# First loads of an encoder layer in halves over two queues, and one accumulating transfer in place of two

## Chip, cores and metric

The kernel runs on one core of one Trainium2 chip. The metric is device microseconds of one execution, taken over several runs. The engines are named as in the profile: PE is the matmul engine, PEld its weight load, DVE the vector engine, ACT the scalar engine, POOL the general-purpose engine, SP the engine that here only issues transfers. A name with a trailing q (SPq, ACTq, POOLq) is the instruction queue of that engine.

## What is computed

One layer of an encoder trunk over 512 positions and 1024 channels, in float32:

```python
def swiglu(h, w_gate, w_up, w_down):
    return (jax.nn.silu(h @ w_gate) * (h @ w_up)) @ w_down

x = x + 0.5 * swiglu(rms_norm(x, ffn1_norm), ffn1_w_gate, ffn1_w_up, ffn1_w_down)
h = rms_norm(x, mix_norm)
u = h @ w_in
f_out = fourier_mixer(u[..., :o0], fnet_w, fnet_b)
a_out = gqa_attention(u[..., o0:o1], u[..., o1:o2], u[..., o2:], q_norm, k_norm)
x = x + jnp.concatenate([f_out, a_out], axis=-1) @ w_out
x = x + 0.5 * swiglu(rms_norm(x, ffn2_norm), ffn2_w_gate, ffn2_w_up, ffn2_w_down)
return rms_norm(x, final_norm)
```

The inner width of both feed-forward parts is 2752, which is 21 blocks of 128 and one of 64.

## The kernel before

Activations lie transposed: `x[k]` is channel block k (128 partitions) by 512 positions, and all of x, after 32 columns of gains, is one tile `gx`. For precision each float32 operand of a matmul is split into a high part, rounded to the matmul's format, and a low part, the remainder. A product of two split operands takes three matmuls (high by high, high by low, low by high). The high part is made by ACT (a cast), the low part by DVE (line 141, a subtraction), or, for some tiles, by a transfer: in `rest_by_dma` ACT writes the negated high part into the low tile (line 172) and POOL issues a transfer from the raw float32 data that adds to it (line 175), in `pieces` column pieces. Split weights lie in slots of one tile, `ring`.

**The opening.** Line 749 on, before the first feed-forward part. `raws[i]` (tile `raw_first`) holds, for two channel blocks, the first four 128-wide chunks of the gate and up weights: [128, 2, 4, 128]. ACT issues two transfers for `raws[0]` (line 751), one for each channel block, 256 KB each. PE runs nine matmuls on a constant (line 757, tile `busy`). SP issues x in five blocks (`load_x`, line 770): block 0 is the gains and `x[0]` (272 KB), block 1 is `x[1]` (256 KB), blocks 2 to 4 are two channel blocks each (512 KB), and in between the weights `raws[1]` to `raws[3]` (line 776, 512 KB each). In `opening1`, for each channel block k, `highs` makes the high parts of x (line 225 on DVE for k = 0, line 227 on ACT otherwise) and of the weights (line 798 on ACT; for k = 0 in two halves, chunks 0 to 1 and chunks 2 to 3), DVE makes the low parts (lines 231 and 141), and `products(k)` issues twelve matmuls (line 812): four chunks high by high, then four high by low, then four low by high. The order of ACT and DVE in the opening is written out by hand; the order of PE and SP is that of the program. What is not written out is ordered by a planner from modelled costs.

**The feed-forward parts.** `ffn` runs four groups of inner blocks. The first group, two or three blocks and the 64-wide rest, is computed plainly by `gate` (lines 201 and 187). The later groups go by `seven`: for each inner block, gate and up are computed as a two-by-two block product with seven multiplications instead of eight. `prepare(j)` returns the steps that make a block's seven weight operands: `ld` (SP loads `raw_g` and `raw_u`, line 398), `a.h` (the high parts of a11 and a12, ACT, line 409), `a.l` (their low parts, `low`, by `rest_by_dma` in two pieces of 256 KB: one for a11, one for a12), `c1` to `c4` (sums on DVE, line 424), and so on. A product `P0` to `P9` is four pairs of matmuls (lines 454 and 457). `P0` uses a11, so it reads what the first piece of `a.l` wrote; `P1` uses a12.

After each group its down projection runs (tile `dn`, line 201; weights from `raw_dn`, cast at line 187). While the down projection of a group runs, the steps of the first block of the next group are issued ahead, in program order between its rounds (`ahead`), and the load of the second block:

```python
if d == (1 if gi else 2) and not last:
    ready = [prepare(groups[gi + 1][0] + i) for i in (1, 2)]
    ahead.extend(ready[0][n] for n in FIRST)
    ahead.append(ready[1]["ld"])
```

So there are six first blocks, three in each feed-forward part. In the middle of the kernel the mixing stage runs in an order written out by hand for all engines. The program gives the transfers of SP and ACT eight completion counters in turn, so that the issue of the ninth waits until the first has landed.

Of the kernel before, what the change touches and what calls it, by code (L numbers as in the profile page):

```python
# [15 lines left out]
P = 128  # L16
S = 512
D = 1024
KD = D // P
# [21 lines left out]
HALF = S // 2  # L41
# [53 lines left out]
def asf(ap):  # L95
    return ap.bitcast(F32)
# [3 lines left out]
def encoder(ctx, tc, A, out):  # L100
    nc = tc.nc
# [18 lines left out]
    def bank(name):  # L120
        return pp.tile([P, S], F32, tag="bank", name=name)


    gx = cp.tile([P, 4 * KD + KD * S], F32, name="gx")
    gains = gx[:, : 4 * KD].rearrange("p (n k) -> p n k", k=KD)
    xt = gx[:, 4 * KD :].rearrange("p (k s) -> p k s", s=S)
    x = [xt[:, k, :] for k in range(KD)]
# [12 lines left out]
    def lows(lo, src, hi):  # L140
        return nc.vector.tensor_tensor(out=lo, in0=src, in1=asf(hi), op=ALU.subtract)  # L141
# [28 lines left out]
    def rest_by_dma(lo, hi, src, pieces=1):  # L170

        nc.scalar.activation(lo, asf(hi), AF.Copy, scale=-1.0)  # L172
        n = lo.shape[-1] // pieces
        for c in (slice(i * n, (i + 1) * n) for i in range(pieces)):
            nc.gpsimd.dma_start(out=lo[..., c], in_=src[..., c], accum_op=ALU.add)  # L175
# [123 lines left out]
    def ffn(norm, after, wgu, wd, wdt, groups, opening, closing):  # L299
# [6 lines left out]
        with tc.tile_pool(name=f"act{n_}", bufs=1) as ap, tc.tile_pool(name=f"sums{n_}", bufs=2) as sp:  # L306
# [5 lines left out]
            wt, raws = [], {}  # L312
# [61 lines left out]
            def back(ts):  # L374
                plain[:] = [t for t in plain if all(t is not q for q in ts)]

            def take():

                t = next(t for t in own or plain if any(t is q for q in own or shared))
                for q in own, shared:  # L380
                    q[:] = [p for p in q if p is not t]
                taken.append(t)
                return t
# [3 lines left out]
                    taken[:] = [q for q in taken if q is not t]  # L387
                    (shared if any(t is q for q in slots[KD:]) else own).append(t)

            def prepare(j):  # L390

                ops, w, t = {}, {}, {}

                def load():
                    t["g"] = sp.tile([P, KD * P], F32, tag="raw_g", name=f"raw_g{n_}_{j}")
                    t["u"] = wp.tile([P, KD * P], F32, tag="raw", name=f"raw_u{n_}_{j}")
                    for r, c in ((t["g"], 2 * j), (t["u"], 2 * j + 1)):
                        nc.sync.dma_start(out=r.rearrange("p (a b) -> p a b", b=P), in_=wgu[c])

                def high(names, src):  # L400
                    if len(names) == 2:
                        hi, lo = (take() for _ in range(2))
                        last = max(names, key=USES.index)
                        w[last, "slots"] = hi, lo
                    else:
                        both = take()
                        hi, lo = both[:, :S], both[:, S:]
                        w[names[0], "slots"] = (both,)
                    nc.scalar.copy(hi, src())  # L409
                    for i, n in enumerate(names):  # L410
                        w[n] = tuple(t[:, i * S : (i + 1) * S] for t in (hi, lo))
                    t[names] = lo, hi

                def low(names, src):
                    lo, hi = t[names]
                    if names[0] in BY_DMA:
                        rest_by_dma(lo, hi, src(), 2)
                    else:
                        lows(lo, src(), hi)

                def combine(tag, c, a, b, op):
                    if c == 0:
                        t[tag] = sp.tile([P, 2 * S], F32, tag=tag, bufs=1, name=f"{tag}_{n_}_{j}")
                    nc.vector.tensor_tensor(out=t[tag][:, c : c + S], in0=a(), in1=b(), op=op)

                a11, a12, a21, a22, s1, s2, s3 = (
                    (lambda r=r, c=c: t[r][:, c : c + S])
                    for r, c in (("g", 0), ("g", S), ("u", 0), ("u", S), ("s12", 0), ("s12", S), ("s34", 0))
                )
                for k, names, src in (  # L430
                    ("a", ("a11", "a12"), lambda: t["g"]), ("s", ("s1", "s2"), lambda: t["s12"]), ("d", ("a22",), a22),
                    ("t", ("s3", "s4"), lambda: t["s34"]),
                ):
                    ops[f"{k}.h"] = lambda names=names, src=src: high(names, src)
                    ops[f"{k}.l"] = lambda names=names, src=src: low(names, src)
                ops["c1"] = lambda: combine("s12", 0, a21, a22, ALU.add)
                ops["c2"] = lambda: combine("s12", S, s1, a11, ALU.subtract)
                ops["c3"] = lambda: combine("s34", 0, a11, a21, ALU.subtract)
                ops["c4"] = lambda: combine("s34", S, a12, s2, ALU.subtract)
                ops["ld"] = load  # L440
                return {**ops, "w": w}
# [165 lines left out]
            def by_tokens(ps, c, group):  # L607

                t = slice(c * P, (c + 1) * P)
                for i in range(LAST):  # L610
                    nc.tensor.matmul(
                        ps[:, i * P : (i + 1) * P], x[KD - LAST + i][:, t], ident, is_transpose=True,
                        start=i == 0, stop=False, skip_group_check=True,
                    )
                for j in group:
                    h, l = (at[:, where[j], o, t] for o in range(2))
                    whi, wlo = (w[:, j - group[0]] for w in tw)
                    for a, b in ((h, whi), (l, whi), (h, wlo)):
                        nc.tensor.matmul(
                            turned(ps[:, : LAST * P]), a, turned(b), start=False, stop=j == group[-1] and b is wlo,  # L620
                            skip_group_check=True,
                        )
                    yield
# [16 lines left out]
            for gi, group in enumerate(groups):  # L640
# [9 lines left out]
                else:  # L650
# [9 lines left out]
                    for i, c in enumerate(left):  # L660
                        pss.setdefault(c // 2, []).append(gate(c, by_dma=i in (1,) if n_ else i > 0))
                        if due:
                            j = due.pop(0)
# [20 lines left out]
                for d in range(KD):  # L684
                    if last and closing and d == KD - LAST:
                        closing(
                            [(e, down(e, group, gi)) for e in range(d, KD)], residual,
                            lambda ps, c: by_tokens(ps, c, group), finished,
                        )
                        break  # L690
                    if last and d == KD - 2:
                        back(lent)
                    ps = bank(f"dn{n_}_{d}_{gi}")
                    while len(downs) < min(d + 1 + (0 if gi or not n_ else 2), KD):
                        downs.append(behind(lambda: down(len(downs), group, gi)))
                    steps = downs[d](ps, every)
                    for _ in range(len(group) - (last and d < 2) - HELD * (d == KD - 1 and not last)):
                        next(steps)
                    waiting.append((d, ps, steps))
                    if d == (1 if gi else 2) and not last:  # L700
                        ready = [prepare(groups[gi + 1][0] + i) for i in (1, 2)]
                        ahead.extend(ready[0][n] for n in FIRST)
                        ahead.append(ready[1]["ld"])
                    if d == 0:
                        rest()
                        if last:

                            lent = slots[KD - 2 : KD]
                            plain[0:0] = lent
                            continue  # L710
                    def finish(waiting=waiting, added=added if last or d < KD - 1 else lambda d, ps: residual(d, ps, every)):
                        for d_, ps, steps in waiting:
                            for _ in steps:
                                pass
                            added(d_, ps)

                    if d < KD - 1 or last:
                        finish()
                    waiting = []
# [27 lines left out]


    raws = [wp.tile([P, 2, 4, P], F32, tag="raw", name=f"raw_first{i}") for i in range(KH)]
    for a in range(2):  # L750
        nc.scalar.dma_start(out=raws[0][:, a], in_=A["first0"][a])


    one = [nc.const_aps.tensor(1.0, [P, n], BF16) for n in (P, S)]
# [7 lines left out]

    n0, n1 = Norm(0), Norm(1)

    cut = [0] + [4 * KD + k * S for k in (1, 2, 4, 6, 8)]

    def load_x(i):
        a, b = cut[i : i + 2]
        src = A["x"][a * P : b * P].rearrange("(p n) -> p n", p=P)
        nc.sync.dma_start(out=gx[:, a:b], in_=src)  # L770

    load_x(0)
    load_x(1)
    for i in range(1, KH):
        load_x(i + 1)
        nc.sync.dma_start(out=raws[i], in_=A["first"][i - 1])
# [74 lines left out]
    with tc.tile_pool(name="mix", bufs=1) as mp, tc.tile_pool(name="mixt", bufs=1) as mt:  # L851
# [49 lines left out]
        raws, ws = {}, {}  # L901
# [757 lines left out]
```

## Time and profile before

| | us |
|---|---|
| median of 3 runs | 813.91 (813.85 to 814.01) |
| the profiled execution's own time | 813.67 |
| its span, first to last instruction | 811.9 |
| PE busy | 805.0 (99% of the span) |
| DVE busy | 642.5 (79%) |
| ACT busy | 546.7 (67%) |
| POOL busy | 109.3 (13%) |

Times in the views are microseconds from the start of the span. The profiled execution's time is 1.8 us more than its span, and 0.24 us under the median of the runs. A busy PE is counted from the start to the modelled end of its matmuls, which overlap; what counts here is where it is not busy. In a view of the timeline a row gives start, length, engine, line, operation, the tile written and the tiles read, how many instructions were merged, and in brackets the idle time before the row and what ended it.

### The profile page before, as it was taken

The page shows a single profiled execution, that of the slowest core. Times are in us where ns is not written, and L with a number is a line of the kernel's source. Part 1 is how long each engine was busy: PE and PEld are TensorE (multiplying, and loading weights), DVE is VectorE, ACT ScalarE, POOL GpSimd, SP SyncE. Part 2 cuts the span into 40 slices and gives each one's busy share as a digit, 9 for nine tenths or more (in the row PEclk, how much of TensorE's full clock was granted, in tenths as well). Part 3 has the DMA queues.
Part 4 walks back from the last instruction along what each step waited for, and adds up shares of the span by engine and source line. Part 5 has one row for each costly group of instructions (what it writes and reads, how often), then busy time and mean ns, then how long its engine had stood idle before and what let it go on. Part 6 is the DMA issues. An engine that isn't in the chain of part 4 may idle for free.

```text
span 811.9 us, 11937 instructions
## 1 busy us (share of the span) xinstructions
PE 805.0 (99%) x4376; PEld 705.4 (87%) x4376; DVE 642.5 (79%) x1077; ACT 546.7 (67%) x871; POOL 109.3 (13%) x124
## 2 busy tenths in 40 slices
PE   9999999999999999999999999999999999999997
PEld 7888988888888888889988888888888888889887
DVE  7996998389765967799998588989883998489774
ACT  7774876278635845779999557568743876278562
POOL 0120220022001200211000001212100220022001
PEclk9999999999999999999999999999999999999999
DMA  7775875558474743352110316678573785558432
GB/s 260 176 164 167 182 175 154 158 136 187 125 208 95 144 125 117 105 172 80 55 52 27 105 52 162 139 195 199 114 208 105 173 185 141 163 130 180 112 97 104
DMA packets 44955, 114.25 MB, mean 141 GB/s; under 512 B 5216, under 2 KB 10720, under 8 KB 44896
## 3 DMA queue, kind: packets, MB, share of 16 engines
q1 hardware_dynamic: 25184, 75.33, 29.8%
q0 software_dynamic: 16400, 29.90, 20.9%
q10 hardware_dynamic: 3312, 8.26, 3.3%
q8 instruction: 34, 0.56, 0.3%
q14 instruction: 25, 0.20, 0.1%
HBM read 84.24 MB, written 2.10 MB: 106 GB/s over the span
## 4 chain that ended last, share of the span: by engine, by line
PE 92%; DVE 4%; DMA 2%; issue 1%; ACT 1%; POOLq 0%; POOL 0%; DVEq 0%; ACTq 0%
PE dn L201 25%; PE r L454 15%; PE mix L201 9%; PE r L457 8%; PE p L454 4%; PE c L454 4%; PE q L454 4%; PE gu L201 3%; PE gu L812 3%; PE p L457 2%; PE q L457 2%; PE c L457 2%; PE mix L1312 2%; PE mix L1272 2%; PE mix L1110 1%
## 5 line engine op out<-in xcount | busy, mean ns | idle before, releaser
L201 PE MATMUL dn<-at,ring 128*128 128x512 f32 x900 | 203.5, 380 | 0.3 <-ACT ring L187 0.3
L201 PEld LDWEIGHTS dn<-at,ring 128*128 128x128 f32 x900 | 167.6, 188 | 29.6 <-ACT ring L187 0.7
L454 PE MATMUL r<-rt,ring 128*128 128x512 f32 x560 | 190.8, 382 | 0.0
L457 PE MATMUL r<-rt,ring 128*128 128x256 f32 x560 | 153.0, 273 | 0.0
L454 PEld LDWEIGHTS r<-rt,ring 128*128 128x128 f32 x560 | 105.1, 188 | 18.7
L457 PEld LDWEIGHTS r<-rt,ring 128*128 128x128 f32 x560 | 105.2, 188 | 0.4
L175 POOL DMA_DIRECT2D ring<-raw_g x70 | 61.0, 1026 | 274.9 <-ACT ring L172 143.0
L635 DVE SCALAR_TENSOR_TENSOR gx<-dn,gx 128x512 f32<-128x512 f32 x61 | 41.7, 686 | 66.3 <-PE dn L201 66.3
L141 DVE TENSOR_TENSOR ring<-s,ring 128x1024 fp32r<-128x1024 f32 x70 | 85.3, 1219 | 2.5 <-ACT ring L409 0.6
L409 ACT CAST ring<-s 128x1024 fp32r<-128x1024 f32 x70 | 73.0, 1043 | 7.8 <-PE p L454 5.6
L187 ACT CAST ring<-raw_dn 128x768 fp32r<-128x768 f32 (+3 forms) x58 | 44.9, 780 | 48.8 <-PE dn L201 35.9
L141 DVE TENSOR_TENSOR ring<-raw_dn,ring 128x768 fp32r<-128x768 f32 (+3 forms) x58 | 51.4, 891 | 15.4 <-ACT ring L187 14.5
L172 ACT ACTIVATE ring<-ring 128x1024 fp32r<-128x1024 f32 x38 | 40.3, 1060 | 14.2 <-PE dn L201 12.5
L201 PE MATMUL gu<-ring 128*128 128x512 f32 x216 | 48.9, 381 | 0.0
L454 PE MATMUL p<-rt,ring 128*128 128x512 f32 x140 | 48.5, 382 | 0.0
L454 PE MATMUL q<-rt,ring 128*128 128x512 f32 x140 | 48.3, 382 | 0.0
L454 PE MATMUL c<-rt,ring 128*128 128x512 f32 x140 | 48.3, 382 | 0.0
L490 ACT COPY p<-r 128x512 f32<-128x512 f32 x35 | 19.9, 570 | 41.2 <-PE r L457 41.2
L201 PEld LDWEIGHTS gu<-ring 128*128 128x128 f32 x216 | 40.4, 188 | 6.9
L409 ACT CAST ring<-raw_g 128x1024 fp32r<-128x1024 f32 x35 | 36.7, 1049 | 11.3 <-DMA raw_g<-in_wgu 11.2
L457 PE MATMUL p<-rt,ring 128*128 128x256 f32 x140 | 38.3, 274 | 0.0
L457 PE MATMUL q<-rt,ring 128*128 128x256 f32 x140 | 38.2, 273 | 0.0
(284 smaller groups left out, 1685.2 us busy)
## 6 DMA issues: line engine op xcount, KB each, us to landing
raw_g<-in_wgu SPq DMA_DIRECT2D x35, 512.0 KB, 4.1
raw_u<-in_wgu SPq DMA_DIRECT2D x35, 512.0 KB, 5.3
ring<-raw_g POOLq DMA_DIRECT2D x70, 256.0 KB, 6.4
raw_dn<-in_wd SPq DMA_DIRECT2D x25, 384.0 KB, 3.3
raw_gu<-in_wgu SPq DMA_DIRECT2D x12, 512.0 KB, 3.6
at<-u POOLq DMA_DIRECT2D x23, 256.0 KB, 3.3
raw_dn<-in_wd ACTq DMA_DIRECT2D x15, 384.0 KB, 3.3
raw_o<-in_wo SPq DMA_DIRECT2D x8, 512.0 KB, 3.4
```

The lines of the kernel that those rows point to most:

```text
L141: return nc.vector.tensor_tensor(out=lo, in0=src, in1=asf(hi), op=ALU.subtract)
L172: nc.scalar.activation(lo, asf(hi), AF.Copy, scale=-1.0)
L175: nc.gpsimd.dma_start(out=lo[..., c], in_=src[..., c], accum_op=ALU.add)
L187: cast["ACT"] = nc.scalar.copy(hi[:, :n, :], raw[:, :n, :])
L201: nc.tensor.matmul(ps, a, b, start=first and b is mhi and a is whi, stop=last and a is wlo)
L409: nc.scalar.copy(hi, src())
L454: nc.tensor.matmul(turned(ps), whi[:, ks], turned(m), start=first and i == 0, stop=False, skip_group_check=True)
L457: nc.tensor.matmul(turned(ps[:, :HALF]), wlo[:, ks], turned(m[:, :HALF]), start=False, stop=i == KH - 1, skip_group_check=True,)
L490: nc.scalar.copy(o[key], o["r"])
L635: nc.vector.scalar_tensor_tensor(out=x[d][:, t], in0=ps[:, t], scalar=0.5, in1=x[d][:, t], op0=ALU.mult, op1=ALU.add)
L812: nc.tensor.matmul(turned(pss[c]), w[:, k % 2, c], turned(m[k]), start=k == 0 and m is hh and w is hi, stop=k == KD - 1 and w is lo,)
L1272: nc.tensor.transpose(pts[n][:, c * P : (c + 1) * P], prob[t, b, c][:, kc * P : (kc + 1) * P], ident)
```

## The change

Two edits.

In the opening, block 0 of x with the gains and the first channel block of `raws[0]` are each cut in two. SP issues the gains with the first 256 positions of `x[0]` (144 KB), then chunks 0 to 1 of the weights (128 KB). ACT issues the other 256 positions (128 KB), then chunks 2 to 3 (128 KB), and then, as before, the second channel block of `raws[0]` (256 KB). `load_x` moves up in the text and gets the queue and the columns as arguments. The rest of the loads follow in the same order as before.

In `prepare`, the first of the two blocks that are prepared ahead (i = 1) has its `a.l` in one transfer of 512 KB instead of two of 256 KB. This holds for the six first blocks; all others keep two.

```diff
-            def prepare(j):
+            def prepare(j, early=False):
...
-                        rest_by_dma(lo, hi, src(), 2)
+                        rest_by_dma(lo, hi, src(), 1 if early else 2)
...
-                        ready = [prepare(groups[gi + 1][0] + i) for i in (1, 2)]
+                        ready = [prepare(groups[gi + 1][0] + i, i == 1) for i in (1, 2)]
...
     raws = [wp.tile([P, 2, 4, P], F32, tag="raw", name=f"raw_first{i}") for i in range(KH)]
-    for a in range(2):
-        nc.scalar.dma_start(out=raws[0][:, a], in_=A["first0"][a])
+    cut = [0] + [4 * KD + k * S for k in (1, 2, 4, 6, 8)]
+
+    def load_x(i, by=nc.sync, t=slice(0, None)):
+        a, b = cut[i : i + 2]
+        src = A["x"][a * P : b * P].rearrange("(p n) -> p n", p=P)
+        by.dma_start(out=gx[:, a:b][:, t], in_=src[:, t])
+
+    early = slice(0, 4 * KD + HALF), slice(4 * KD + HALF, None)
+    for by, t, c in zip((nc.sync, nc.scalar), early, (slice(0, 2), slice(2, 4))):
+        load_x(0, by, t)
+        by.dma_start(out=raws[0][:, 0, c], in_=A["first0"][0][:, c])
+    nc.scalar.dma_start(out=raws[0][:, 1], in_=A["first0"][1])
...
-    cut = [0] + [4 * KD + k * S for k in (1, 2, 4, 6, 8)]
-
-    def load_x(i):
-        a, b = cut[i : i + 2]
-        src = A["x"][a * P : b * P].rearrange("(p n) -> p n", p=P)
-        nc.sync.dma_start(out=gx[:, a:b], in_=src)
-
-    load_x(0)
     load_x(1)
     for i in range(1, KH):
         load_x(i + 1)
```

## The prediction

> **What bounds the kernel now.** I read the page's shares first, then the chain that ended last, then the waits of PE, and then the opening by timeline. The page:
>
> ```profile
> span 811.9 us, 11937 instructions
> PE 805.0 (99%) x4376; PEld 705.4 (87%) x4376; DVE 642.5 (79%) x1077; ACT 546.7 (67%) x871; POOL 109.3 (13%) x124
> ```
>
> PE is idle for 6.9 us in all. Busy time in stretches (start and end, length, then PE busy) says where:
>
> ```profile
> 0.00:5.03 5.03, 3.82 (x9) 1.17 (x10) 0.84 (x7) 1.95 (x4) 0.70 (x6) 1.00 0.64 200
> 5.03:28.00 22.97, 22.97 (x109) 19.49 (x110) 19.98 (x30) 18.39 (x30) 1.53 (x1) 1.00 0.72 253
> 345.00:500.00 155.00, 154.92 (x897) 136.53 (x896) 130.91 (x237) 123.69 (x225) 9.70 (x9) 1.00 0.27 86
> 500.00:800.00 300.00, 299.72 (x1643) 264.20 (x1642) 236.25 (x388) 194.84 (x298) 45.88 (x52) 1.00 0.61 148
> 800.00:811.90 11.90, 6.60 (x44) 6.27 (x43) 4.89 (x11) 2.55 (x7) 2.86 (x5) 0.91 0.49 176
> ```
>
> Idle are 1.21 us in the opening, 0.36 us from 5.03 to 800, and 5.3 us in the tail, which the change does not touch. So what moves the first product moves the end by as much, and between the opening and the tail there is next to nothing to win. The first entries of the chain (start, length, what) and the waits of PE over the whole kernel:
>
> ```profile
> 0.74 3.81 DMA raw_first<-in_first
> ...
> 4.57 0.41 ACT ring L798
> ...
> 5.03 17.89 PE gu L812 x80
> ...
> PE busy L757 <- PEq L1642: 0.8, 1, 0.8
> PE gu L812 <- ACT ring L798: 0.4, 1, 0.4
> PE dn L201 <- ACT ring L187: 0.3, 1, 0.3
> ```
>
> The opening is bounded by the landing of the first weights and their cast, and the constant matmuls before it cap the gain:
>
> ```profile
> 0.78 3.82 PE L757 MATMUL busy<-const-bfloat16-1.0 128*128 128x512 bf16 x9 [0.78 <-PEq L1642]
> 4.40 0.48 DVE L225 TENSOR_SCALAR ring<-gx 128x512 fp32r<-128x512 f32 x1 [3.28 <-DMA gx<-in_x]
> 4.57 0.71 ACT L798 CAST ring<-raw_first 128x256 fp32r<-128x256 f32 x2 [1.41 <-DMA raw_first<-in_first]
> 5.51 0.72 ACT L227 ACTIVATE ring<-gx 128x512 fp32r<-128x512 f32 x1 [0.23 <-DMA gx<-in_x]
> ```
>
> The nine end at 4.60. The high part of x is done at 4.88, the first half cast at 4.98, the first product starts at 5.03. The gap is 0.43 us, so the first product can come at most 0.43 us earlier, 0.05% of the time. About 0.2% (1.6 us) is what a measurement of this kernel can tell from no change.
>
> **The opening, by bytes.** Before, ACT's first transfer (262 kB, rows of 2 KB) and SP's first (279 kB, rows of 2176 B) run at once. After, each queue has half of x and then half of the weights: SP 147 + 131 kB, ACT 131 + 131 kB. That is the same count of bytes on each queue ahead of the last byte needed. x lands earlier, but the cast that was last waits for the weights, which now come second. The issue costs nothing itself: SP's second issue starts some 0.4 us after its first, long before the first one's bytes have gone. What remains is the rate, since the rows are now 1024 and 1152 B. Three stretches, with the busy share of the transfer engines and the GB/s at the end of the row: 3 to 4 us (rows of 2 KB, the opening), 6 to 8 us (rows of 4 KB), and 497.5 us, where only a transfer of 1 KB rows runs (`raw_dn`, 128 KB):
>
> ```profile
> 3.00:4.00 1.00, 1.00 (x4) 0.31 (x3) 0.00 (x0) 0.16 (x1) 0.00 (x0) 1.00 1.04 394
> 6.00:8.00 2.00, 2.00 (x10) 1.69 (x9) 1.84 (x4) 1.47 (x3) 0.00 (x0) 1.00 1.01 412
> 497.50:498.00 0.50, 0.50 (x4) 0.44 (x3) 0.50 (x2) 0.50 (x2) 0.00 (x0) 1.00 0.66 205
> q1 hardware_dynamic: 109, 0.20, 54.1%
> q10 hardware_dynamic: 106, 0.19, 49.6%
> ```
>
> The last two rows are the queues of SP and ACT between 3 and 4 us: they share the engines evenly, so neither half overtakes the other by its queue. At a full share, rows of 1 KB run at 205 / 0.66 = 311 GB/s. The 541 kB take 1.37 us at 394 GB/s and 1.74 us at 311; the 147 kB in rows of 1152 B are a little quicker, so I count 1.72 us, 0.35 us more.
>
> The Trainium skill, "DMA: Bandwidth & Descriptors", section "Why small descriptors are slow (HBM only)", puts the price at about 3 cycles of bus a packet beside one for each 32 B: an estimate of 35/67 for 1 KB against 2 KB, 4.5% a byte, or 0.06 us here, by which the sum would be about 0.15 us earlier than before. The trace disagrees: from 2 KB to 1 KB rows the rate falls by 21%.
>
> Where the SP half landed, if bytes alone counted: x block 0 was issued at 0.74 and landed 3.6 us later:
>
> ```profile
> gx<-in_x SPq DMA_DIRECT2D x1, 272.0 KB, 3.6
> gx<-in_x SPq DMA_DIRECT2D x1, 256.0 KB, 4.2
> raw_first<-in_first ACTq DMA_DIRECT2D x2, 256.0 KB, 4.2
> ```
>
> So SP's half of the weights, which ends the same 279 kB, lands at 4.34 at the old rate and at 4.69 at the new. The cast of half the weights takes 0.41 us (4.57 to 4.98) and PE follows 0.05 later: 4.82 or 5.17. That is -0.21 or +0.14 us. I take +0.1, near the dearer value, because its row is of the same row length. The bounds: below, -0.43 (the constant matmuls). Above, the halves land like the transfer that was issued second on SP before (`x[1]`, issued at about 1.15, 4.2 us to landing, 5.37): cast to 5.78, product at 5.83, +0.80. ACT's half, 4.55 + 0.35 = 4.90, is cast behind the first half (which ends at 5.10), and is wanted two matmuls after the first product, 0.44 us later: hidden.
>
> **What else the opening moves.** One more issue on ACT (0.45 us) lies ahead of its table load; ACT was idle for 1.41 us before the cast, so it is covered. SP's later loads come behind one more issue, and in the new order the ninth transfer is `x` block 3 instead of block 4; the wait of the ninth for the first, seen before, moves there:
>
> ```profile
> SPq L770 <- DMA raw_first<-in_first: 0.8, 1, 0.8
> 2.60 0.62 SPq L770 DMA_DIRECT2D gx<-in_x  x1
> 3.26 0.46 SPq L776 DMA_DIRECT2D raw_first<-in_first  x1
> 4.56 0.33 SPq L770 DMA_DIRECT2D gx<-in_x  x1
> 12.36 0.71 ACT L227 ACTIVATE ring<-gx 128x512 fp32r<-128x512 f32 x1
> 12.97 0.60 ACT L798 CAST at<-raw_first 128x512 fp32r<-128x512 f32 x1
> ```
>
> Block 3 would be issued at some 3.9 (when the first half of x lands) instead of 2.60, `raws[2]` at some 4.7 instead of 3.26, block 4 at some 5.1 instead of 4.56. Queued behind are only loads; the bytes ahead of them, 1.6 MB on SP's queue and 0.5 MB on ACT's, keep the engines full until about 8 us, so a later issue leaves no hole. Their first users stand at 12.36 and 12.97. If that cover were gone, 1.3 us of delay would stand against the 0.43 us gap of the first wait. The nearest users are tighter: `x[1]` is scaled at 5.51 after a wait of 0.23 for its landing, and its weights are cast until 6.74, while PE reaches channel block 1 at 5.03 + 12 x 0.22 = 7.7. Delayed by the 0.35 us of the rate, 0.6 us are left. DVE's first three steps start earlier or wait for the same cast.
>
> **The six accumulating transfers.** The edit takes out 6 of 70 issues on POOL (about 0.87 us each) and a landing each. POOL is 13% busy. One transfer of 512 KB was seen only from the weights in memory: 5.3 and 5.7 us to landing. The pairs took, by the group and by single places:
>
> ```profile
> ring<-raw_g POOLq DMA_DIRECT2D x70, 256.0 KB, 6.4
> ring<-in_wgu POOLq DMA_DIRECT2D x3, 512.0 KB, 5.3
> at<-in_wgu POOLq DMA_DIRECT2D x1, 512.0 KB, 5.7
> 523.12 1.78 POOL L175 DMA_DIRECT2D ring<-raw_g  x2 [10.54 <-ACT ring L187]
> L175 POOL DMA_DIRECT2D ring<-raw_g x2: 900/1038/1176, 523.1 to 523.7; - x2
> DMA to landing us min/median/max: 3.4/4.2/5.0
> 533.80 0.38 PE L454 MATMUL r<-rt,ring 128*128 128x512 f32 x1
> 534.02 0.27 PE L457 MATMUL r<-rt,ring 128*128 128x256 f32 x1
> ```
>
> The last five rows are of the tightest of the six places, the second group of the second feed-forward part: issue at 523.12, first piece down 3.4 us later, the second 5.0 us after its own issue at 523.7. P0 starts at 533.80 and its first matmul with the low part at 534.02. So the first piece had 7.5 us to spare, and one piece that takes 5.7 us has 5.2. `raw_g` comes free at about 528.8 instead of 528.7, so the next load of SP, which waits for it, moves by a tenth either way. Cost: zero, hidden by the last rounds of the down projection; if that cover were gone, each place would cost what the piece is late.
>
> **Sum.** 813.67 (profiled) + 0.1 + 0 = 813.8 for an execution like the profiled one; against the median, 813.91 + 0.1 = 814.0.
>
> **Rivals.**
>
> 1. The opening gains. Rows of 1 KB are no slower when two queues feed the engines, and the halves land earlier, so the first product starts between 4.60 and 4.85: 813.5 to 813.7. For it: ACT and DVE both waited only for landings. Against it: the row at 311 GB/s, and that the weights stand second on both queues. By the Trainium skill's price per packet, above, it would be 813.8.
>
> 2. The halves land late, as a second issue did: +0.80, 814.7. For it: 4.2 us to landing in both such rows. Against it: in those rows the time is that of the bytes ahead.
>
> 3. Slower, by one mechanism: the 512 KB piece lands after P0. Place: the P0 of the first block in the second feed-forward part, at 534.02. It decides from 10.9 us after the issue on, and each us beyond is a us at the end; 12.6 us give 815.6. For it: P0 needs the whole transfer where it needed half. Against it: nothing from POOL took over 8.8 us:
>
> ```profile
> DMA to landing us min/median/max: 3.3/6.3/8.8
> ```
>
> 4. Planned order. ACT and DVE in the first group and beside the down projections are ordered from modelled costs, and these change with both edits. A cast of 1.05 us ahead of the one that PE waited 0.3 us for would cost up to 1.05 us: 814.9. The traces cannot exclude it.
>
> **How the numbers follow.** My forecast (814.0, between 813.7 and 814.2) has 0.62, rival 1 0.15, rival 2 0.10, rival 3 0.04, rival 4 0.09, of which 0.02 beyond 1.6 us in all. The range of 8 in 10 reaches to rivals 1 and 2: 813.4 (813.91 - 0.43, less the spread of 0.1 between runs) to 814.8 (814.71 + 0.1). Faster by over 0.2% has 0.02: no idle time of PE before the tail is that large, so it would have to come from the tail. Slower by over 0.2% has 0.06, rivals 3 and 4. Within 0.2%: 0.92.
>
> **What would show it.** In the profile after, x's first operation on DVE (line 225) before 4.2, with the first cast (line 798) still at 4.4 to 4.8 behind a landing of `raw_first`; the first product at 4.8 to 5.2; no wait of PE on line 454 or 457; 64 transfers of 256 KB and 6 of 512 KB at line 175. I am wrong if the first cast starts by 4.2 (then the order of the bytes does not count as I think), if PE waits in channel blocks 1 or 2, or if a wait on line 187 grows past 0.3 us.

## The result, and the profile after

| | before | after |
|---|---|---|
| median of the runs, us | 813.95 (8 runs) | 816.27 (8 runs) |
| the profiled execution, us | 813.67 | 816.2 |
| its span, us | 811.9 | 814.4 |

The change makes the kernel slower: the ratio is 1.0032, 95% interval 1.0021 to 1.0042, and the medians lie 2.3 us apart. The 816.27 us lie outside the predicted range (813.4 to 814.8).

The page of the kernel after has the same work on PE. POOL's work is less, and the packets on its queue (q0; the columns are packets, MB and share) are fewer. The first three rows are of after, the last is of before:

```profile
span 814.4 us, 11917 instructions
PE 805.4 (99%) x4376; PEld 705.8 (87%) x4376; DVE 642.8 (79%) x1077; ACT 547.0 (67%) x871; POOL 104.0 (13%) x118
q0 software_dynamic: 15536, 29.89, 20.7%
...
q0 software_dynamic: 16400, 29.90, 20.9%
```

Divided by 16 transfer engines, that is 971 packets on each after and 1025 before. This turned out to be the number that matters. First the stretches of after, with PE's busy time second:

```profile
345.00:500.00 155.00, 154.91 (x897) 136.52 (x897) 130.99 (x238) 123.59 (x225) 10.39 (x10) 1.00 0.27 86
500.00:800.00 300.00, 300.00 (x1647) 264.92 (x1645) 236.94 (x389) 195.67 (x299) 43.24 (x49) 1.00 0.60 148
800.00:814.40 14.40, 6.60 (x44) 6.26 (x43) 4.90 (x11) 2.55 (x7) 2.86 (x5) 0.89 0.40 146
```

Against the rows of before: from 500 to 800, PE has no idle time any more (0.28 us before). In the last stretch every engine has the busy time of before (PE 6.60, DVE 4.89, ACT 2.55, POOL 2.86), to 0.01 us, but the stretch is 14.40 us long instead of 11.90. So nothing that computes accounts for the 2.5 us; they lie behind the last work. PE's last matmul starts at 806.33 before and at 806.32 after.

What stands there is found only by asking for the instructions of the program's last line, since a drain is not counted as busy. The rows give the minimum, median and longest duration in ns of the drains of one engine, and when the first and the last start; the longest of POOL's three is the first. The first two are of before, the other two of after:

```profile
L1648 POOLq DRAIN  x3: 40/102/1378, 806.7 to 811.6; - x3
L1648 SPq DRAIN  x3: 7/7/7, 811.1 to 811.4; - x3
...
L1650 POOLq DRAIN  x3: 40/93/6892, 806.7 to 814.1; - x3
L1650 SPq DRAIN  x3: 7/7/7, 810.9 to 813.9; - x3
```

POOL's first closing drain starts at 806.7 in both. Before it takes 1.378 us and ends at 808.1, while SP, which waits for the last stores, comes to its own drain at 811.1: the 1.378 us are hidden, with 3.0 us to spare. After it takes 6.892 us and ends at 813.6, 2.7 us later than SP's. All engines then meet, which takes 0.8 us more in both. SP's waits from 807 us on say the same; the first two rows are of before, the last two of after:

```profile
SPq L1648 <- DMA out_y<-y: 1.9, 3, 1.0
SPq L1648 <- PEq L1648: 0.7, 2, 0.5
...
SPq L1650 <- PEq L1650: 3.3, 2, 2.8
SPq L1650 <- DMA out_y<-y: 1.8, 3, 0.8
```

The wait for the stores is unchanged, the wait in the meeting grew from 0.7 to 3.3 us. The profile names PE's queue as the releaser, but PE's own last matmul starts at 806.3; it is the meeting, which POOL's drain holds up.

The opening and the stall near 529 us changed too, and cancel. The chain in the opening of after:

```profile
1.65 5.33 DMA gx<-in_x
...
7.07 0.72 ACT ring L227
7.79 0.52 ACT ring L800
...
8.35 15.25 PE gu L814 x68
...
28.68 26.40 PE gu L201 x120
```

And its timeline:

```profile
3.66 0.49 DVE L225 TENSOR_SCALAR ring<-gx 128x512 fp32r<-128x512 f32 x1 [2.54 <-DMA gx<-in_x]
4.20 0.71 ACT L800 CAST ring<-raw_first 128x256 fp32r<-128x256 f32 x2 [0.56 <-DMA raw_first<-in_first]
4.66 3.40 PE L814 MATMUL gu<-ring 128*128 128x512 f32 x12
8.35 1.83 PE L814 MATMUL gu<-ring 128*128 128x512 f32 x7 [0.30 <-ACT ring L800]
```

The first product starts at 4.66 instead of 5.03, but PE then waits for channel block 1, whose `x[1]` landed only at 6.98 (1.65 + 5.33). The first plain group (line 201, 120 matmuls) starts at 28.68; the same row of before has it at 28.00:

```profile
28.00 26.40 PE gu L201 x120
```

So the opening cost 0.68 us. Near 529 us the same 0.68 us come back. The first two rows are of before, the last two of after:

```profile
528.95 0.86 ACT L187 CAST ring<-raw_dn 128x256 fp32r<-128x256 f32 x2 [3.77 <-PE dn L201]
529.40 0.95 PE L201 MATMUL dn<-at,ring 128*128 128x512 f32 x3 [0.28 <-ACT ring L187]
...
528.95 0.73 ACT L187 CAST ring<-raw_dn 128x256 fp32r<-128x256 f32 x2 [3.03 <-DMA raw_dn<-in_wd]
529.57 0.84 PE L201 MATMUL dn<-at,ring 128*128 128x512 f32 x3
```

After, PE is later by the opening's 0.68 us and no longer waits for this cast. From PE's matmul number 2800 to number 3500, counted by their starts, it takes 127.12 us instead of 127.80. So in these two executions +0.68 and -0.68 cancel, and the end is left: +2.5.

### The profile page after: what moved, and what is told of

It reads as the page before. It is cut to its first block, busy times and chain, and to the rows that moved or that the text cites. A ratio compares the mean times of both kernels' runs of the same rounds, so it can differ in the third digit from the quotient of the medians.

```text
span 814.4 us, 11917 instructions
## 1 busy us (share of the span) xinstructions
PE 805.4 (99%) x4376; PEld 705.8 (87%) x4376; DVE 642.8 (79%) x1077; ACT 547.0 (67%) x871; POOL 104.0 (13%) x118
## 3 DMA queue, kind: packets, MB, share of 16 engines
q0 software_dynamic: 15536, 29.89, 20.7%
## 4 chain that ended last, share of the span: by engine, by line
PE 97%; DMA 1%; issue 0%; ACT 0%; DVE 0%; SPq 0%; POOLq 0%; POOL 0%; DVEq 0%; ACTq 0%
PE dn L201 26%; PE r L454 15%; PE mix L201 9%; PE gu L201 8%; PE r L457 8%; PE p L454 4%; PE c L454 4%; PE q L454 4%; PE gu L814 2%; PE p L457 2%; PE q L457 2%; PE c L457 2%; PE mix L1314 2%; PE mix L1274 2%; PE mix L1114 1%; PE mix L1112 1%
## 5 line engine op out<-in xcount | busy, mean ns | idle before, releaser
L175 POOL DMA_DIRECT2D ring<-raw_g x64 | 55.7, 1015 | 278.9 <-ACT ring L172 194.2
```

## The experiments

In the tables, "drain" is POOL's first closing drain, "packets" are those on POOL's queue for each transfer engine, and "block 1" is the start of PE's first product of channel block 1.

**Which of the two edits.** e1 has the new opening and all pairs in two pieces; e2 has the old opening and the six pieces.

```diff
 e1 (from after)
-                        rest_by_dma(lo, hi, src(), 1 if early else 2)
+                        rest_by_dma(lo, hi, src(), 2)
 e2 (from before)
-                        rest_by_dma(lo, hi, src(), 2)
+                        rest_by_dma(lo, hi, src(), 1 if early else 2)
-                        ready = [prepare(groups[gi + 1][0] + i) for i in (1, 2)]
+                        ready = [prepare(groups[gi + 1][0] + i, i == 1) for i in (1, 2)]
```

> The opening alone; all accumulating transfers stay in two pieces. Theory 1 (POOL's closing drain grew because of the accumulating transfers): the drain lasts about 1.4 us as before and the time is within 1 us of before; the first product still starts near 4.66 and channel block 1 waits for x[1] as in the changed kernel, so PE is some 0.7 us late at 28 us. Theory 2 (the opening sets the end, and the drain only shows something late): about 816.2, with the long drain of 6.9 us.

> The accumulating transfers alone (six pairs in one piece); the opening is that of before. Theory 1: the drain lasts 6.9 us and the time is 815.6 to 816.3. Theory 2: the drain lasts 1.4 us and the time is 813.9 or, if the wait of PE for a cast at 529 goes, 813.3.

e1: 814.69 us against 814.01, ratio 1.0012 (1.0003 to 1.0021). e2: 815.88 us, ratio 1.0022 (1.0014 to 1.0031). The drains of e1 and then of e2:

```profile
L1650 POOLq DRAIN  x3: 40/102/1378, 808.1 to 812.9; - x3
...
L1648 POOLq DRAIN  x3: 40/93/6891, 806.2 to 813.6; - x3
```

The long drain belongs to the pieces, and the opening has no part in it. In e2's profile the last matmul starts at 805.78, 0.55 us earlier than before; the drain eats that and 2 us more. In e1's it starts at 807.68, 1.35 us later than before: 0.85 us of this are there where the first plain group starts (28.85 against 28.00), and 0.51 us come between matmul 2800 and 3500 (128.31 us).

**Which of the six places.** e3 has the one piece in the first feed-forward part only, e4 in the second only, e5 in one place of the second, e6 in one place of the first.

```diff
+                        ready = [prepare(..., i == 1 and not n_) for i in (1, 2)]              # e3
+                        ready = [prepare(..., i == 1 and n_) for i in (1, 2)]                  # e4
+                        ready = [prepare(..., i == 1 and n_ and gi == 0) for i in (1, 2)]      # e5
+                        ready = [prepare(..., i == 1 and not n_ and gi == 0) for i in (1, 2)]  # e6
```

> One piece at the three places of the first feed-forward part only (102 transfers from POOL instead of 105 and 99). If the length of the drain follows the count of POOL's transfers in proportion, it is about 4.1 us (and hidden behind the stores, which end the kernel at about 811 when the drain is under some 4.3 us): time as before. If it follows a threshold or something done late in the kernel: 1.4 or 6.9.

> One piece at the three places of the second feed-forward part only (102 transfers). By count alone the drain is the same as with the three places of the first part; if the long drain comes from the late one-piece transfers themselves, it is 6.9 us here and 1.4 us with the first part's. The wait of PE at 529 goes if one piece is what takes it away.

> One piece at one place only, the first block of the second group of the second feed-forward part (104 transfers from POOL). If the late raw_dn landing at 529 is what the pair of transfers causes, the wait of PE there goes and PE ends 0.4 to 0.7 us earlier. The drain: if it grows with each transfer taken away (1.4 at 105, 5.2 or 7.1 at 102, 6.9 at 99), 1.4 to 5; under some 4.3 us it is hidden and the time is 813.4; else 814 to 815.5.

> One piece at the first place of the first feed-forward part only (104 transfers). If the drain is set by the count alone, it is as long as with one place in the second part; if by where in the order of POOL's transfers the longer one stands, it differs. PE keeps a wait of 0.3 to 1.2 us at 529.

| | transfers of POOL | packets | drain, us | drain ends | SP's drain starts | span | time |
|---|---|---|---|---|---|---|---|
| e3 | 102 | 998 | 5.176 | 811.50 | 810.67 | 812.28 | 814.05 (one run) |
| e4 | 102 | 998 | 7.056 | 813.09 | 810.37 | 813.88 | 815.65 (one run) |
| e5 | 104 | 1016 | 5.259 | 811.76 | 810.84 | 812.54 | 814.42, ratio 1.0006 (0.9997 to 1.0015) |
| e6 | 104 | 1016 | 5.302 | 812.27 | 811.30 | 813.05 | 814.82 (one run) |

One single transfer less, in whichever part, is enough to lengthen the drain from 1.4 to 5.3 us. In which part the transfer stands is therefore not what makes the drain long. In each row the span is 0.8 us more than the end of the drain. e4 and e3 have the same number of packets but drains of 7.1 and 5.2 us; what sets the length within the long kind was not found.

**The sum of POOL's queue.** e7 is the kernel before with two small loads moved from SP to POOL (107 transfers). e8 is the kernel after with six transfers of another stage cut in two, so that POOL's queue has the sum of before.

```diff
 e7 (from before)
-        nc.sync.dma_start(out=qkg, in_=A["qkg"])
-        nc.sync.dma_start(out=fb, in_=A["fb"])
+        nc.gpsimd.dma_start(out=qkg, in_=A["qkg"])
+        nc.gpsimd.dma_start(out=fb, in_=A["fb"])
 e8 (from after)
-                    f["nh"] = lambda: rest_by_dma(o["at"][1], o["at"][0], o["u"])
+                    f["nh"] = lambda: rest_by_dma(o["at"][1], o["at"][0], o["u"], 2 if j % 6 == 4 else 1)
```

> The kernel before with the two small loads qkg and fb issued by POOL instead of SP, so 107 transfers from POOL and none in one piece. If the drain follows the position that POOL's transfers have reached, it is not 1.4 us although no accumulating transfer was changed; if only the one-piece transfers lengthen it, it stays at 1.4.

> The changed kernel with six other accumulating transfers (three in each feed-forward part, the low part of an activation, 256 KB) cut in two of 128 KB, so that POOL issues 105 again. If the drain follows the count of transfers, 1.4 us and a time of about 814; if the one-piece transfers of 512 KB lengthen it, about 6.9 us and 816.3.

e7: 813.31 us, drain 1.492. e8: 813.62 us, drain 1.380, with all six transfers of 512 KB in place (one run each):

```profile
L1650 POOLq DRAIN  x3: 40/102/1380, 806.7 to 811.6; - x3
```

So neither the size of the pieces nor the edit as such makes the drain long.

In e7 and e8 the number of transfers and the number of packets move together. e9 and e13 separate them. e9 has the one-piece transfers of e2, and two constant tables of POOL are stored with gaps so that their loads fall into shorter packets. e13 has them too, but issues each of the six as two transfers of 64 partitions with uncut rows.

```diff
 e9 (from e2)
-            for t, n in ((chan, "chan"), (pos, "pos"), (both, "both")):
-                nc.gpsimd.dma_start(out=t, in_=A[n])
+            nc.gpsimd.dma_start(out=chan, in_=A["chan"][:, :, :P])
+            nc.gpsimd.dma_start(out=pos.rearrange("p (a b) -> p a b", a=8), in_=A["pos"][:, :, :225])
+            nc.gpsimd.dma_start(out=both, in_=A["both"])
...
+    pos = np.pad(pos.reshape(P, 8, 225), ((0, 0), (0, 0), (0, 31)))
+    chan = np.pad(chan, ((0, 0), (0, 0), (0, P)))
 e13 (from e2)
-    def rest_by_dma(lo, hi, src, pieces=1):
+    def rest_by_dma(lo, hi, src, pieces=1, halves=False):
...
-            nc.gpsimd.dma_start(out=lo[..., c], in_=src[..., c], accum_op=ALU.add)
+            if pieces == 1 and halves:
+                for r in (slice(0, 64), slice(64, P)):
+                    nc.gpsimd.dma_start(out=lo[r], in_=src[r], accum_op=ALU.add)
+            else:
+                nc.gpsimd.dma_start(out=lo[..., c], in_=src[..., c], accum_op=ALU.add)
...
-                        rest_by_dma(lo, hi, src(), 1 if early else 2)
+                        rest_by_dma(lo, hi, src(), 1 if early else 2, early)
```

> The one-piece transfers alone (99 transfers issued by POOL, whose closing drain took 6.9 us), with two of POOL's constant tables stored with gaps, so that their loads fall into shorter packets: still 99 transfers, but about 1050 packets on each of the queue's engines where the one-piece kernel had 971 and the kernel before 1025. Theory that the packets of POOL's whole queue set the closing drain, with a step between 1016 and 1025 on each engine: the drain is 1.4 to 1.5 us and the time 813.3 to 813.6 us, about as before or 0.5 us faster. Rival that the number of transfers sets it (99 to 104 long, 105 and more short): the drain stays 5 to 7 us and the time 815.4 to 816.2 us.

> The one-piece transfers alone, but each of the six issued as two transfers of 64 partitions each with rows uncut: POOL issues 105 transfers as the kernel before does, in 971 packets an engine as the one-piece kernel does. Theory that packets set the closing drain: it stays long, 5 to 7 us, and the time is 815.2 to 816.2 us. Rival that the count of transfers matters too: 1.4 to 1.6 us and 813.2 to 813.9 us.

The packets and the drain of e9, then of e13:

```profile
q0 software_dynamic: 16816, 29.89, 21.1%
L1653 POOLq DRAIN  x3: 40/102/1584, 806.8 to 811.8; - x3
...
q0 software_dynamic: 15632, 29.90, 21.4%
L1652 POOLq DRAIN  x3: 40/102/7260, 809.4 to 817.2; - x3
```

e9 has 99 transfers, as the slow kernels, but 1051 packets an engine, and its drain is short, a little above the 1.4 to 1.5 us expected: 813.73 us, ratio 0.9998 (0.9989 to 1.0008). e13 has 105 transfers, as before, but 977 packets, and its drain is the longest of all: 819.29 us in its one run. In both, short or long came out as the theory of packets had it. The number of transfers does not decide, the packets do. e13's time missed its expectation (815.2 to 816.2): in this run PE was late too, with its longest wait near 532 us:

```profile
532.13 0.49 PE L205 MATMUL dn<-at,ring 128*128 128x512 f32 x1 [2.02 <-ACT ring L191]
```

**Versions that keep the sum.** e10 has the old opening, the six pieces, and e8's edit; e15 is e8 again, now timed.

> The opening of before, the six one-piece transfers, and six other accumulating transfers (those of the activations, every sixth) cut in two, so that POOL issues 105 transfers and 1025 packets an engine as before. Theory (the loss is POOL's closing drain, the gain of the one-piece transfers is the stall near 529 us): drain 1.4 us, no stall at 529, 813.2 to 813.8 us, 0.2 to 0.7 us faster than before. Rival that 512 KB transfers make the drain long by themselves: drain 5 to 7 us, 815.4 to 816.2 us. Second rival that the stall at 529 is chance and not the second piece: 813.9 us, no difference.

> The whole change, and six of the activations' accumulating transfers cut in two, so that POOL's queue has the 1025 packets an engine of before. Theory that of the change's 2.3 us nearly all is POOL's closing drain, and that the later block 1 (0.6 us) and the shorter stall near 529 us (0.5 us) about cancel: 813.4 to 814.2 us, not to be told from before. Rival that the opening costs what the opening alone cost (0.7 to 1.0 us) and nothing comes back: 814.5 to 814.9 us.

e10: 813.45 us median, against 813.86; ratio of the runs compared 0.9999 (0.9991 to 1.0008). e15: 814.30 against 814.05, ratio 1.0007 (0.9997 to 1.0016). The drain and PE from 500 to 800 us in e10:

```profile
L1648 POOLq DRAIN  x3: 40/93/1380, 805.9 to 810.8; - x3
500.00:800.00 300.00, 300.00 (x1647) 265.20 (x1646) 235.64 (x387) 194.03 (x297) 45.75 (x52) 1.00 0.61 148
```

With the packets back, the whole change is not to be told from before, though e15's interval reaches 1.3 us; and e2, which has the long drain without the new opening, cost 1.9 us. So most of the 2.3 us are the drain. What the opening costs on the average stays open: e1 says 0.7 us, and e15's median is 0.25 us above that of before, 0.1 us over the range expected.

e10's profile shows the better version as argued (no stall, short drain, last matmul at 805.52 instead of 806.33), but its time is not shown to be better than before. In the profiles the time from matmul 2800 to 3500 was 127.06 to 127.62 us where the second part's first pair is one piece, and 127.06 to 128.31 where it is two (e13, with its split rows, aside). e7, with two pieces, lost nothing there, and e5 and e8, with one, lost about 0.5 us near 528. The one piece has the shorter times more often, but that it takes the stall away is not shown.

**The two halves of the opening.** e11 has only x in halves: the first weights are whole, on ACT's queue behind the second half of x. e12 has only the weights in halves: x is whole on SP's queue, ahead of SP's half of the weights.

```diff
 e11
+    for by, t in zip((nc.sync, nc.scalar), early):
+        load_x(0, by, t)
+    for a in range(2):
+        nc.scalar.dma_start(out=raws[0][:, a], in_=A["first0"][a])
 e12
+    load_x(0)
+    for by, c in zip((nc.scalar, nc.sync), (slice(0, 2), slice(2, 4))):
+        by.dma_start(out=raws[0][:, 0, c], in_=A["first0"][0][:, c])
+    nc.scalar.dma_start(out=raws[0][:, 1], in_=A["first0"][1])
```

> Of the opening only one part: the first block of x in two halves on SP's and ACT's queues; the first weights whole on ACT's queue behind the second half of x; accumulating transfers as before. Theory that the weights' order is what makes the second block of x late: with the weights' halves gone from SP's queue the second block of x lands near 5.4 us, channel block 1 starts at 7.8 us, and the first product comes at 4.9 to 5.3 us as before; 813.7 to 814.3 us. Rival that the split of x makes it late: block 1 starts at 8.2 to 8.5 us as in the full opening, 814.4 to 814.9 us. Rival that the late start is chance from run to run: block 1 lies anywhere from 7.8 to 8.4 us.

> The other part of the opening: the first block of x whole on SP's queue, the first weights in two halves (ACT's queue first, SP's queue behind x); accumulating transfers as before. Theory that the weights' half on SP's queue ahead of the second block of x is what makes that block late: block 1 starts at 8.2 to 8.5 us and the time is 814.4 to 814.9 us; the first product at 4.5 to 5.1 us. Rival that the split of x makes it late: block 1 at 7.8 us and 813.6 to 814.2 us.

e11: 815.48 us, ratio 1.0028 (1.0016 to 1.0040). e12: 813.96 us, ratio 1.0002 (0.9993 to 1.0011). The first cast and PE's wait for it in e11, then the same cast and the products in e12:

```profile
6.40 0.71 ACT L800 CAST ring<-raw_first 128x256 fp32r<-128x256 f32 x2 [2.75 <-DMA raw_first<-in_first]
PE gu L814 <- ACT ring L800: 2.1, 1, 2.1
...
4.26 0.91 ACT L800 CAST ring<-raw_first 128x256 fp32r<-128x256 f32 x2 [1.10 <-DMA raw_first<-in_first]
4.72 4.62 PE L814 MATMUL gu<-ring 128*128 128x512 f32 x18
```

e11 missed all three of its expectations: its weights landed at 6.4, so the first product moved to 6.86, and block 1 to 12.14. Its profiled execution is the slowest of its five (818.53 us), 3.05 us above their median, so these waits need not be those of the other four. A half of x ahead of whole weights was dear here; with the weights in halves too, the first product of e1 came at 4.52. In e12 PE runs through from 4.72 (block 1 at 7.86, no wait), and the time is that of before, so SP's half of the weights does not by itself make block 1 late; that theory fell.

## Why the prediction was wrong, point by point

**The tail: this step failed.** The prediction wrote of the tail's 5.3 us "which the change does not touch". It looked at PE's idle time there and did not ask which queue reaches the program's end last. POOL's drain was a hidden item of 1.378 us; it grew to 6.892 us and stuck out by 2.7. The six transfers were costed "zero, hidden by the last rounds of the down projection", at the place where they are issued; their cost is at the end of the program and comes with the number of packets on POOL's queue.

**The six transfers where they run.** Right: no wait of PE on lines 454 or 457, so rival 3 did not occur. These are PE's waits and the pieces after:

```profile
PE busy L767 <- PEq L1644: 0.8, 1, 0.8
PE gu L814 <- ACT ring L800: 0.3, 1, 0.3
...
ring<-raw_g POOLq DMA_DIRECT2D x58, 256.0 KB, 6.8
ring<-raw_g POOLq DMA_DIRECT2D x6, 512.0 KB, 5.9
```

The one piece takes 5.9 us to landing where 5.3 to 5.7 were assumed. The prediction's own list said 64 transfers of 256 KB beside the six; it is 64 in all. That the wait on line 187 was absent after, worth 0.68 us in this execution, was not foreseen; the experiments do not show that the edit is the reason.

**The opening by bytes: mis-sized.** The weights' half was put at 4.69 us, because rows of 1 KB ran at 311 GB/s when alone. Here is the stretch from 3 to 4 us of after, in which 312 of 364 packets are under 2 KB:

```profile
DMA packets 364, 0.38 MB, mean 379 GB/s; under 512 B 46, under 2 KB 312, under 8 KB 364
3.00:4.00 1.00, 1.00 (x4) 0.31 (x3) 0.34 (x1) 0.64 (x2) 0.00 (x0) 1.00 1.09 379
raw_first<-in_first SPq DMA_DIRECT2D x1, 128.0 KB, 3.0
```

It moved 379 GB/s, 4% less than the 394 of before and not 21%. SP's half, issued at 1.19, landed 3.0 us later at 4.2. The price from a single short transfer did not hold with both queues full. Nor is the rate the whole of it: from 2 to 3 us the rate was 244 GB/s against 150 before, so the bytes also began to flow sooner, and the prediction had no term for that. The Trainium skill, "DMA: Bandwidth & Descriptors", section "Why small descriptors are slow (HBM only)", by whose price per packet the estimate was 4.5%, came nearer: the trace shows 4% by the rates, and 8% when each is divided by its busy share (1.09 and 1.04). Rival 1 had this right for the first product, and the first cast at 4.20 was the sign that the prediction itself had named for being wrong.

**What else the opening moves: mis-sized.** "Delayed by the 0.35 us of the rate, 0.6 us are left" for `x[1]`. It was delayed by 1.6 us (1.65 + 5.33 after, about 1.15 + 4.2 before): 0.5 us by the later issue, which the prediction put at nothing, and 1.1 us by a longer way to landing. The rate of after and then of before between 5 and 6 us:

```profile
5.00:6.00 1.00, 1.00 (x4) 0.78 (x4) 0.64 (x1) 0.00 (x0) 0.00 (x0) 1.00 0.89 244
q1 hardware_dynamic: 56, 0.21, 79.5%
...
5.00:6.00 1.00, 0.97 (x4) 0.86 (x5) 1.00 (x2) 0.77 (x2) 0.00 (x0) 1.00 1.07 434
q1 hardware_dynamic: 92, 0.36, 88.6%
```

The rate is 244 GB/s instead of 434. A packet of SP's queue took 0.795 x 16 / 56 = 0.227 us of an engine, against 0.886 x 16 / 92 = 0.154. Why they are slower stays open. It also varies: with this opening, block 1 started at 8.35 (after), 8.39 (e1), 7.85 (e8) and 7.62 us (e15); with the old one at 7.66 to 7.99, and at 8.34 in e13.

**Rivals and chances.** Rival 2 (late halves) did not occur, and of rival 4 (another planned order) no wait of PE was seen. "Slower by over 0.2%" got 0.06, for rivals 3 and 4; it came by a mechanism that the list lacked. Without the drain, the sum of the parts (+0.68 and -0.68) would have ended at 813.67, within the range by two errors that cancel.

## What to carry to other kernels

Before costing an edit that changes how many transfers an engine issues, read the drains at the program's end: which engine's queue closes last, and how much the others have to spare. A hidden 1.4 us became a visible 6.9 us with 54 packets fewer on each engine, and six cuts in an unrelated stage hid it again. A term that frees an idle engine is not free until the end of the program has been looked at.

## What the hardware showed that was not expected

Whether POOL's closing drain is short or long goes, in these 16 kernels, with the packets that its queue has moved in the whole program, not with what is still under way, nor with the bytes (29.89 to 29.90 MB in all 16). In after, no packet of q0 is among those from 759 us to 806 us, when the drain starts:

```profile
q1 hardware_dynamic: 1555, 3.17, 20.8%
q10 hardware_dynamic: 576, 1.18, 7.5%
q8 instruction: 2, 0.03, 0.3%
q14 instruction: 3, 0.02, 0.1%
```

| packets an engine | drain, us | kernels |
|---|---|---|
| 971 | 6.89 | after, e2 |
| 977 | 7.26 | e13 |
| 998 | 5.18 and 7.06 | e3, e4 |
| 1016 | 5.26 and 5.30 | e5, e6 |
| 1025 | 1.38 | before, e1, e8, e10, e11, e12, e15 |
| 1029 | 1.49 | e7 |
| 1051 | 1.58 | e9 |

The step lies between 1016 and 1025. Each kernel has one profiled execution, but the seven with 1025 packets agree within 0.002 us. In before and in after the first 0.6 us of the drain are POOL's own last operation, which ends at 807.3.

One transfer of 128 partitions is 9 packets an engine here (1025 - 1016, with one transfer less). By the Trainium skill, "DMA: Bandwidth & Descriptors", section "The descriptor swizzle", a transfer of 1 MiB from POOL to 128 partitions makes nine on each engine, eight of data and one of completion. The trace agrees: 1680 of before's 16400 packets are of 4 bytes, one for each of 105 transfers on each of 16 engines. Whether these small packets count is not separated: without them, the step lies between 912 and 920.

Above the step the drain grows slowly with the packets (1.38, 1.49 and 1.58 us); below it no order is seen. Why there is a step, and what the long drains pay for, stays open. The kernel before stood at most nine packets, one transfer, above it.
